# A hybrid attention and convolution block: later transposes of k and q tiles, and one filler part moved ahead of the attention

## The chip, the cores and the metric

One NeuronCore of a Trainium2 chip runs the whole program. The metric is device time in microseconds, the median of several executions of the same kernel. The engines are PE (matmuls and transposes; PEld loads its weights), DVE, ACT and POOL (vector work), and SP, whose queue issues all DMAs here.

## The reference, cut to what matters

One layer over 1024 tokens of width 1024. Everything is float32. The change lies in the first half, up to the output projection:

```python
h = rmsnorm(x, attn_norm)
q, k, v, conv_a, conv_g = split(h @ w_in)           # 512 columns each
q = rmsnorm(q.reshape(S, 4, 2, 64), q_norm)         # k likewise
o = diff_attention(q, k, v, lam)                    # 4 heads, two softmax maps each, ALiBi bias
attn_out = rmsnorm(o, head_norm) * (1 - lam_init)
conv_out = silu(layernorm(depthwise_conv31(conv_a * sigmoid(conv_g))))
x = x + concat([attn_out, conv_out]) @ w_out
# then a SwiGLU feed-forward part and a gated per-layer embedding, both added to x
```

## The kernel before, in words

Each float32 product is made of three matmuls on parts rounded to the PE's input format: high by high, low by high and high by low (`mm3`, lines 78 to 80). So every operand is split into a high and a low tile, the high one by ACT, the low one by DVE or POOL.

Tokens are worked on in 8 tiles of 128. The stages up to the attention are: a norm of x with transposes, v and a small projection of the per-layer embedding; the convolution channels (GLU, 31 taps, layer norm, swish), with the k projection beside their end; and the q projection, beside the layer norm of the convolution. `qk_proj` makes the k and the q tiles. For token tile t it does 24 matmuls into a PSUM tile `pk` or `pq`; ACT copies it to `nk` or `nq` and squares it; DVE sums the squares (`ssk`, `ssq`), POOL raises the sums to the power -1/2 (`rstd_of`, line 107), DVE multiplies; PE transposes the tile (`tk`, `tq`, line 376); ACT and DVE write the halves `qh` and `ql` (lines 379, 380); and two DMAs store them to DRAM, from where the attention loads them per head.

The attention has 16 parts: 4 heads by 2 halves of the queries by 2 pairs of query tiles. For a query tile, PE makes the scores of each of two maps (`s`, lines 562 to 565), DVE takes the negative maximum (`nm`), ACT the exponential (`e`, line 570), POOL combines the two maps (lines 578, 579), PE transposes the result in two halves (`wt`, line 584), ACT and DVE split it (`wth`, `wtl`), and PE multiplies it with v (`av`). Two PSUM tiles hold scores, two hold transposes. A head's result is normed by `head_norm` (transposes `hn` and `hb`), a head's half later.

The convolution's share of the output projection, `conv_out(i)`, fills PE between the attention's steps: 16 pieces `pc` of 12 matmuls each, for 2 column halves by 8 token tiles, each with a residual `pt` loaded from x, an addition and a store to `part_d`. Part i of the attention issues piece i, after its last scores. `conv_w` loads the weights (`wcr`) and splits them (`wch`, `wcl`). After the attention comes the projection of its own result, `po`, with the weights `wo`.

The order of instructions on each engine is fixed when the program is built, by a scheduler that goes by the order of the code, by priorities (`later`, `issue_after`) and by a modelled timeline; on the chip each engine takes its instructions in that order. `issue_after(x)` makes the instructions inside it eligible only once x has been issued.

Of the kernel before, what the change touches and what calls it, by code (L numbers as in the profile page):

```python
# [2 lines left out]

# [5 lines left out]
F32 = mybir.dt.float32  # L9
F32R = mybir.dt.float32r  # L10
BF16 = mybir.dt.bfloat16
AF = mybir.ActivationFunctionType
ALU = mybir.AluOpType
AX = mybir.AxisListType
# [3 lines left out]
P = 128  # L18
# [19 lines left out]
NVF = 4  # L38
ND = [23, 17, 17, 18]
OTB = 2  # L40
FSTART = 0
HNT = (0, 3)
NVL = 2
MV = (0, 0)
# [7 lines left out]
def hybrid_block(ctx: ExitStack, tc: tile.TileContext, I, out):  # L52
# [6 lines left out]
    def f32(ap):  # L59
        return ap.bitcast(F32)  # L60
# [15 lines left out]
    def mm3(ps, lh, ll, rh, rl, first, last, more=False):  # L76

        nc.tensor.matmul(ps, lh, rh, start=first, stop=False, skip_group_check=more)  # L78
        nc.tensor.matmul(ps, lh, rl, start=False, stop=False, skip_group_check=more)  # L79
        nc.tensor.matmul(ps, ll, rh, start=False, stop=last, skip_group_check=more)  # L80

    @contextmanager
    def later(n):
# [20 lines left out]
    def rstd_of(ms, n, pool, name):  # L104
        r = pool.tile([P, n], F32, name=name + "_r", tag="st_r", bufs=4)
        nc.vector.tensor_scalar_add(ms, ms, EPS)  # L106
        nc.gpsimd.tensor_tensor(r, ms, mhalf[:, 0:1].broadcast_to([P, n]), ALU.pow)  # L107
        return r
# [45 lines left out]
    def mm_tile(name):  # L154
        i = mmn[0] = (mmn[0] + 1) % mmn[1]
        if i < 2:
            return ps1.tile([P, 512], F32, name=name, tag=f"mm{i}", bufs=1)
        return psB.tile([P, 512], F32, name=name, tag=("av", "fl")[i - 2], bufs=1)
# [33 lines left out]
    def proj_tok(ps, t, ws):  # L192
        half, tt = t // 4, t % 4
        a = slice(tt * P, (tt + 1) * P)
        for k in range(KT):
            wh, wl = ws(k)
            mm3(ps, hT[half][k // 4][:, k % 4, a], lT[half][k // 4][:, k % 4, a], wh, wl, k == 0, k == KT - 1)

    wv_load, wv = w_set(rp1, [(wq[i], 2) for i in (0, 1, 2, 3)], w_in, 2 * CW, "wv", 3, nc.gpsimd)

# [121 lines left out]
    def conv_tile(j, ndve, delay):  # L322
# [19 lines left out]
        with later(delay):  # L342
# [13 lines left out]
                    nc.gpsimd.tensor_add(y2, y2, pr)  # L356
            nc.vector.tensor_add(y, acc, y2)

    def qk_proj(nm, c0, g, hd, ld, slots):
        load, ws = w_set(rp1, [(wq[i], 2) for i in slots], w_in, c0, "w" + nm, 3, nc.vector)  # L360
        for i in range(4):
            load(i)
        for t in range(NT):
            ps = mm_tile(f"p{nm}{t}")
            proj_tok(ps, t, ws)
            qn = p1m.tile([P, 8, HD], F32, name=f"n{nm}{t}", tag="sq", bufs=7)
            nc.scalar.copy(qn.rearrange("p a b -> p (a b)"), ps)
            sq = p1m.tile([P, 512], F32, name=f"sq{nm}{t}", tag="sq", bufs=7)
            nc.scalar.activation(sq, ps, AF.Square, scale=HD ** -0.5)
            ss = p1m.tile([P, 8], F32, name=f"ss{nm}{t}", tag="qss", bufs=4)  # L370
            nc.vector.tensor_reduce(ss, sq.rearrange("p (a b) -> p a b", b=HD), AX.X, ALU.add)
            r = rstd_of(ss, 8, p1m, f"r{nm}{t}")
            nc.vector.tensor_mul(qn, qn, r.unsqueeze(2).broadcast_to([P, 8, HD]))
            tp = tp_tile(f"t{nm}{t}")
            for h in range(NH):
                nc.tensor.transpose(tp[:, h, :], qn[:, 2 * h:2 * h + 2, :], ident)
            qh = nat.tile([P, NH, P], F32R, name=f"{nm}h{t}", tag="nat", bufs=6)
            ql = nat.tile([P, NH, P], F32R, name=f"{nm}l{t}", tag="nat", bufs=6)
            nc.scalar.activation(qh, tp, AF.Copy, scale=g)
            nc.vector.scalar_tensor_tensor(ql, tp, g, f32(qh), ALU.mult, ALU.subtract)  # L380
            for dst, src in ((hd, qh), (ld, ql)):
                c0 = t * P % dst[0].shape[1]
                dma(f32(dst[t // 4][:, c0:c0 + P]).rearrange("(h p) s -> p h s", p=P), f32(src))

    def conv_ln():

# [65 lines left out]
                split(wh[:, k, :], wl[:, k, :], raw, None, (nc.gpsimd, nc.vector)[ch == 0 and 2 * g + k in WV])  # L452
            woc.append((wh, wl))

    def conv_out(i):

        ch, t = i // NT, i % NT
        cs = slice(ch * 512, (ch + 1) * 512)
        if t == 0 and ch == 1:
            conv_w(1, otp, 2, "pt")  # L460
        pt = otp.tile([P, 512], F32, name=f"pt{ch}{t}", tag="pt", bufs=2)
        dma(pt, x[t * P:(t + 1) * P, cs])
        ps = psB.tile([P, 512], F32, name=f"pc{ch}{t}", tag="fl", bufs=1)
        a = slice(t % 4 * P, (t % 4 + 1) * P)
        for k in range(NCT):
            wh, wl = woc[k // 2]
            mm3(ps, mC[0][t // 4][:, k, a], mC[1][t // 4][:, k, a], wh[:, k % 2, :], wl[:, k % 2, :],
                k == 0, k == NCT - 1)
        nc.vector.tensor_add(pt, pt, ps)
        dma(part_d[t * P:(t + 1) * P, cs], pt)  # L470

    mmn[1] = QB
    qk_proj("q", 0, qg, qh_d, ql_d, (2, 3, 0, 1))
    conv_w(0, rp1, 3, "raw")
    es1.close()
    ps1.release()

# [44 lines left out]
    for h in range(NH):  # L522
# [11 lines left out]
        for c in range(2):  # L534
# [14 lines left out]
            for pr_ in range(2):  # L549
# [37 lines left out]
                    if pend and tt in HNT:  # L587
                        next(pend[0], None)
                fi = h * 4 + c * 2 + pr_ - FSTART
                if fi >= 0:  # L590
                    n = 16 - fi if h * 4 + c * 2 + pr_ == 15 else 1
                    with tc.issue_after(s_mm.ins), later(FDELAY):
                        for i in range(fi, fi + n):
                            conv_out(i)
# [495 lines left out]
```

## Time and profile before

| | us |
|---|---|
| median of 3 executions (lowest, highest) | 1291.48 (1289.46, 1292.21) |
| the profiled execution, its own time | 1289.18 |
| the span of its trace | 1287.4 |
| PE busy in the span | 1249.3 |
| DVE, ACT, POOL busy | 937.5, 583.0, 394.4 |

The span leaves out 1.8 us of the profiled execution. The times in the rows below count from the start of the span. Conv pieces run from 292.7 to 476 us, the k products from 170.4 to 221, the q products from 223.5 to 279.

### The profile page before, as it was taken

How to read it: one execution, taken by the hardware profiler on the slowest of the kernel's cores; microseconds unless marked ns; L12 is line 12 of the kernel's file. 1: busy time of each engine (PE TensorE's matmuls, PEld its weight loads, DVE VectorE, ACT ScalarE, POOL GpSimd, SP SyncE). 2: the span in 40 equal slices, each digit the busy share in tenths (PEclk: the TensorE clock that was granted, in tenths of full speed). 3: DMA queues.
4: the chain of work that ended last, by engine and by line, in shares of the span. 5: the costliest groups of instructions: out<-in, count | busy, mean ns of one | idle time of the engine just before them, and what ended most of it. 6: DMA issues, size and time to landing. Idle time of an engine off the chain costs nothing.

```text
span 1287.4 us, 16537 instructions
## 1 busy us (share of the span) xinstructions
PE 1249.3 (97%) x5945; PEld 1021.1 (79%) x5945; DVE 937.5 (73%) x1220; ACT 583.0 (45%) x862; POOL 394.4 (31%) x237
## 2 busy tenths in 40 slices
PE   8999998989999999987999999999999999999998
PEld 6788877867887888866888888888888788888886
DVE  7548999868887885877667676667665576567797
ACT  7445565445776673442223232223232444346552
POOL 2459998576667661660000000000000000000230
PEclk9999999989999999988999999999999999999999
DMA  9731232496655243445444445444454997665445
GB/s 356 240 88 50 66 107 74 127 225 176 154 126 149 76 134 121 172 131 180 146 165 147 156 164 172 147 161 147 152 171 166 385 349 234 191 196 176 135 147 164
DMA packets 165079, 213.12 MB, mean 166 GB/s; under 512 B 12088, under 2 KB 90182, under 8 KB 164997
## 3 DMA queue, kind: packets, MB, share of 16 engines
q1 hardware_dynamic: 164996, 212.06, 52.0%
q8 instruction: 47, 0.77, 0.3%
q14 instruction: 36, 0.29, 0.1%
HBM read 146.41 MB, written 65.60 MB: 165 GB/s over the span
## 4 chain that ended last, share of the span: by engine, by line
PE 81%; DVE 7%; DMA 6%; issue 2%; POOL 2%; ACT 1%; SPq 1%; DVEq 0%; POOLq 0%; ACTq 0%
PE Y L78 5%; PE Y L79 5%; PE Y L80 5%; PE Z L79 3%; PE Z L78 3%; PE Z L80 3%; PE X L80 3%; PE X L78 3%; PE X L79 3%; PE dY L78 2%; PE dY L79 2%; PE dY L80 2%; PE s L562 2%; DVE acc L351 2%; PE s L563 2%
## 5 line engine op out<-in xcount | busy, mean ns | idle before, releaser
L107 POOL TENSOR_TENSOR n_r<-n_ss,mhalf 128x1 f32<-128x1 f32 x24 | 14.7, 617 | 670.1 <-DVE n_ss L106 661.6
L74 DVE TENSOR_TENSOR dl<-dr,dh 128x1024 fp32r<-128x1024 f32 x77 | 93.7, 1224 | 62.6 <-ACT dh L71 62.4
L71 ACT CAST dh<-dr 128x1024 fp32r<-128x1024 f32 x77 | 80.5, 1049 | 105.9 <-PE dY L80 37.2
L356 POOL TENSOR_TENSOR z<-z,pr 128x1024 f32<-128x1024 f32 x45 | 115.8, 2575 | 3.2 <-ACT pr L355 0.8
L351 DVE SCALAR_TENSOR_TENSOR acc<-u,cw,acc 128x1024 f32<-128x1024 f32 x71 | 91.2, 1285 | 1.5
L570 ACT ACTIVATE e<-s,nm 128x1024 f32<-128x1024 f32 x64 | 71.6, 1119 | 35.9 <-DVE nm L567 29.6
L567 DVE TENSOR_REDUCE nm<-s 128x1 f32<-128x1024 f32 x64 | 77.3, 1219 | 9.1 <-PE s L565 4.5
L579 POOL TENSOR_TENSOR e<-e,e 128x1024 f32<-128x1024 f32 x32 | 77.8, 2431 | 2.4
L355 ACT ACTIVATE pr<-u,cw 128x1024 f32<-128x1024 f32 x45 | 51.1, 1150 | 36.0 <-POOL z L356 35.6
L562 PE MATMUL s<-ka,qa 128*128 128x512 f32 x128 | 57.3, 448 | 1.6 <-ACT e L570 1.5
L578 POOL TENSOR_SCALAR e<-e,cf 128x1024 f32<-128x1024 f32 x32 | 36.9, 1153 | 65.0 <-DVE cf L577 31.9
L79 PE MATMUL dY<-dl,dh 128*128 128x512 f32 x132 | 51.5, 390 | 0.0
L563 PE MATMUL s<-kb,qb 80*128 80x512 f32 x128 | 51.4, 402 | 0.0
L80 PE MATMUL dY<-dh,dl 128*128 128x512 f32 x132 | 51.4, 389 | 0.0
L78 PE MATMUL dY<-dh 128*128 128x512 f32 x132 | 50.3, 391 | 0.0
L74 DVE TENSOR_TENSOR wtl<-wt,wth 128x512 fp32r<-128x512 f32 x64 | 43.2, 683 | 8.9 <-ACT wth L71 8.6
L71 ACT CAST wth<-wt 128x512 fp32r<-128x512 f32 x64 | 36.8, 587 | 20.6 <-PE wt L584 20.5
L796 DVE TENSOR_TENSOR aa<-Z,aa 128x512 f32<-128x512 f32 x22 | 15.2, 690 | 38.5 <-PE Z L80 38.3
L80 PE MATMUL X<-B11h,a11l 128*128 128x512 f32 x88 | 33.5, 401 | 6.5 <-DVE a11l L74 6.5
L79 PE MATMUL av<-wtl,avh 128*128 128x256 f32 x128 | 38.4, 300 | 0.0
L584 PE MATMUL wt<-ident,e 128*128 128x128 f32 x256 | 37.5, 273 | 0.3 <-DVE wtl L74 0.2
L78 PE MATMUL av<-wth,avh 128*128 128x256 f32 x128 | 37.5, 293 | 0.2 <-ACT wth L71 0.2
(396 smaller groups left out, 3984.9 us busy)
## 6 DMA issues: line engine op xcount, KB each, us to landing
dr<-ga_d SPq DMA_DIRECT2D x77, 256.0 KB, 5.6
wr<-in_w_gate SPq DMA_DIRECT2D x44, 256.0 KB, 3.0
wr<-in_w_up SPq DMA_DIRECT2D x44, 256.0 KB, 3.5
wd<-in_w_down SPq DMA_DIRECT2D x22, 512.0 KB, 3.5
wb_d<-wd SPq DMA_DIRECT2D x44, 256.0 KB, 2.0
ga_d<-h SPq DMA_DIRECT2D x44, 256.0 KB, 3.6
dr<-wb_d SPq DMA_DIRECT2D x44, 256.0 KB, 3.4
dr<-in_w_down SPq DMA_DIRECT2D x33, 256.0 KB, 3.1
```

The costliest lines, as they stand in the source:

```text
L71: nc.scalar.copy(h, src)
L74: (eng_l or nc.vector).tensor_sub(l, src, f32(h))
L78: nc.tensor.matmul(ps, lh, rh, start=first, stop=False, skip_group_check=more)
L79: nc.tensor.matmul(ps, lh, rl, start=False, stop=False, skip_group_check=more)
L80: nc.tensor.matmul(ps, ll, rh, start=False, stop=last, skip_group_check=more)
L351: nc.vector.scalar_tensor_tensor(acc, u[:, k:k + S], cw[:, j, k:k + 1], acc, ALU.mult, ALU.add)
L356: nc.gpsimd.tensor_add(y2, y2, pr)
L562: nc.tensor.matmul(o, qa[:, m, ts_], ka[:, m, kc * 512:(kc + 1) * 512], start=True, stop=False)
L563: nc.tensor.matmul(o, qb[:, m, ts_], kb[:, m, kc * 512:(kc + 1) * 512], start=False, stop=not diag)
L567: nc.vector.tensor_reduce(nm, sp, AX.X, ALU.max, negate=True)
L570: nc.scalar.activation(e, sp, AF.Exp, bias=nm, accum_out=s)
L579: nc.gpsimd.tensor_add(es[0], es[0], es[1])
```

## The change

The transposes of a k or q tile, the two splits of them and the two stores become a function `turn`. It isn't called in the turn of its own tile: it is put on a list, and called inside `issue_after` behind the last matmul of a later tile, for k tiles behind two further tiles' products, for q tiles from the second on behind one. The last two k turns come with the first q tiles, and the last q turn comes behind `conv_out(0)`. Piece 0 of `conv_out` is issued before the attention, and its residual is loaded by a statement ahead of the q projection, into a tile of its own. Part i of the attention then issues piece i + 1, and the last part has none.

```diff
-FSTART = 0
+FSTART = -1
...
+    turns = []
+
     def qk_proj(nm, c0, g, hd, ld, slots):
...
-        for t in range(NT):
-            ps = mm_tile(f"p{nm}{t}")
-            proj_tok(ps, t, ws)
...
+        def turn(t, qn):
             tp = tp_tile(f"t{nm}{t}")
...
+        for t in range(NT):
+            ps = mm_tile(f"p{nm}{t}")
+            mm = proj_tok(ps, t, ws)
+            keep = 1 if nm == "k" or t == 0 else 0
+            with tc.issue_after(mm.ins):
+                while len(turns) > keep:
+                    turns.pop(0)()
...
+            turns.append(partial(turn, t, qn))
...
-    def conv_out(i):
+    def conv_out(i, pt=None):
...
-        pt = otp.tile([P, 512], F32, name=f"pt{ch}{t}", tag="pt", bufs=2)
-        dma(pt, x[t * P:(t + 1) * P, cs])
+        if pt is None:
+            pt = otp.tile([P, 512], F32, name=f"pt{ch}{t}", tag="pt", bufs=2)
+            dma(pt, x[t * P:(t + 1) * P, cs])
...
+    pt0 = p1m.tile([P, 512], F32, name="pt00", tag="pt0")
+    dma(pt0, x[0:P, 0:512])
     qk_proj("q", 0, qg, qh_d, ql_d, (2, 3, 0, 1))
     conv_w(0, rp1, 3, "raw")
+    mm = conv_out(0, pt0)
+    with tc.issue_after(mm.ins):
+        turns.pop(0)()
...
-                if fi >= 0:
+                if fi < 16:
```

What this does to the order on the engines is shown at two places. In the names, the digits behind `nq`, `tq`, `qh` are the token tile; those behind `s`, `nm`, `e` are head, query tile and map; those behind `pc` are column half and token tile; those behind `wt` are head, query tile and half; the number after the underscore is a buffer.

**End of the q projection.** PE before, from the transposes of q tile 5 on:

```order
L376 MATMUL tq5_2466<-ident_86,nq5_2456 128x128 x4
L80 MATMUL pq7_2523<-wq3_h_2197,lT11_142 128x512
L376 MATMUL tq6_2512<-ident_86,nq6_2502 128x128 x4
L562 MATMUL s000_2662<-ka0_2641,qa00_2650 128x512
...
L562 MATMUL s001_2673<-ka0_2641,qa00_2650 128x512
...
L376 MATMUL tq7_2558<-ident_86,nq7_2548 128x128 x4
L562 MATMUL s011_2716<-ka0_2641,qa00_2650 128x512
...
L78 MATMUL pc00_2750<-wch00_2569,mCh0_2157 128x512
```

PE in the changed kernel:

```order
L370 MATMUL tq5_2493<-ident_86,nq5_2458 128x128 x4
L80 MATMUL pq7_2514<-wq3_l_2178,hT11_138 128x512
L81 MATMUL pq7_2514<-wq3_h_2177,lT11_142 128x512
L79 MATMUL pc00_2580<-wch00_2560,mCh0_2135 128x512
...
L370 MATMUL tq6_2539<-ident_86,nq6_2504 128x128 x4
L581 MATMUL s000_2679<-ka0_2658,qa00_2667 128x512
...
L370 MATMUL tq7_2595<-ident_86,nq7_2550 128x128 x4
L581 MATMUL s010_2722<-ka0_2658,qa00_2667 128x512
...
L79 MATMUL pc01_2767<-wch00_2560,mCh0_2135 128x512
```

Piece `pc00` moved ahead of the transposes of q tile 6, the transposes of q tile 7 ahead of the third score tile `s010`, and `pc01` stands where `pc00` stood.

ACT before, from the squares of q tile 7 on:

```order
L369 ACTIVATE sqq7_2550<-pq7_2523 128x512
L379 ACTIVATE qh6_2517<-tq6_2512,qg_706 128x512
L570 ACT_TABLE_LOAD
L570 ACTIVATE e000_2670,sm000_2671<-s000_2662,nm000_2668 128x1024
L570 ACTIVATE e001_2681,sm001_2682<-s001_2673,nm001_2679 128x1024
L379 ACTIVATE qh7_2563<-tq7_2558,qg_706 128x512
L570 ACTIVATE e010_2713,sm010_2714<-s010_2705,nm010_2711 128x1024
```

ACT in the changed kernel:

```order
L390 ACTIVATE sqq7_2552<-pq7_2514 128x512
L373 ACTIVATE qh6_2544<-tq6_2539,qg_706 128x512
L373 ACTIVATE qh7_2600<-tq7_2595,qg_706 128x512
L589 ACT_TABLE_LOAD
L589 ACTIVATE e000_2687,sm000_2688<-s000_2679,nm000_2685 128x1024
L589 ACTIVATE e001_2698,sm001_2699<-s001_2690,nm001_2696 128x1024
L589 ACTIVATE e010_2730,sm010_2731<-s010_2722,nm010_2728 128x1024
```

`qh7` moved ahead of the table load and of the first two exponentials. DVE before, from the sum of squares of q tile 7 on:

```order
L371 TENSOR_REDUCE ssq7_2552<-sqq7_2550 128x8
L380 SCALAR_TENSOR_TENSOR ql6_2518<-tq6_2512,qg_706,qh6_2517 128x512
L106 TENSOR_SCALAR ssq7_2552<-ssq7_2552 128x8
L567 TENSOR_REDUCE nm000_2668<-s000_2662 128x1
L567 TENSOR_REDUCE nm001_2679<-s001_2673 128x1
L373 TENSOR_TENSOR nq7_2548<-nq7_2548,rq7_r_2554 128x512
```

DVE in the changed kernel:

```order
L392 TENSOR_REDUCE ssq7_2554<-sqq7_2552 128x8
L107 TENSOR_SCALAR ssq7_2554<-ssq7_2554 128x8
L482 TENSOR_TENSOR pt00_2155<-pt00_2155,pc00_2580 128x512
L374 SCALAR_TENSOR_TENSOR ql6_2545<-tq6_2539,qg_706,qh6_2544 128x512
L394 TENSOR_TENSOR nq7_2550<-nq7_2550,rq7_r_2556 128x512
L586 TENSOR_REDUCE nm000_2685<-s000_2679 128x1
L586 TENSOR_REDUCE nm001_2696<-s001_2690 128x1
L374 SCALAR_TENSOR_TENSOR ql7_2601<-tq7_2595,qg_706,qh7_2600 128x512
```

The scaling of q tile 7 moved ahead of the two maxima, and the addition of piece 0 came in between.

**Last part of the attention.** PE before, from the end of the last score tile `s371` on:

```order
L565 MATMUL s371_4985<-distb_732,identb_730 128x128
L78 MATMUL pc17_5026<-wch10_3959,mCh1_2159 128x512
...
L80 MATMUL pc17_5026<-wch11_3969,mCl1_2160 128x512
L501 MATMUL hn30_4823<-ident_86,ot30_4821 128x128 x4
L584 MATMUL wt350_4873<-ident_86,e350_4852 128x128 x4
L78 MATMUL po00_5306<-wo00_h_5272,mAh0_2637 128x512
...
L584 MATMUL wt351_4880<-ident_86,e350_4852 128x128 x4
...
L78 MATMUL av31_4904<-wth310_4776,avh3_4465 128x256
...
L584 MATMUL wt360_4960<-ident_86,e360_4939 128x128 x4
```

PE in the changed kernel:

```order
L584 MATMUL s371_5002<-distb_732,identb_730 128x128
L520 MATMUL hn30_4840<-ident_86,ot30_4838 128x128 x4
L603 MATMUL wt350_4890<-ident_86,e350_4869 128x128 x4
L603 MATMUL wt351_4897<-ident_86,e350_4869 128x128 x4
L79 MATMUL av31_4921<-wth310_4793,avh3_4482 128x256
L79 MATMUL po00_5306<-wo00_h_5272,mAh0_2654 128x512
...
L603 MATMUL wt360_4977<-ident_86,e360_4956 128x128 x4
```

`pc17` is gone from behind the scores, and the second half of the transposes, `wt351`, and the first `av31` moved ahead of the first matmuls of `po`. In the k stage, the rows of PE are the same in both kernels up to the first q products, so the transposes of k tiles 0 to 5 stand where they stood. On SP, the load of the residual `pt00` moved to the beginning of the program, behind the load of x tile 3.

## Rows read from the trace of the kernel before

**Rows 1.** Page: busy time of the matmul engine; GB/s moved in 40 slices.
```profile
PE 1249.3 (97%) x5945; PEld 1021.1 (79%) x5945; DVE 937.5 (73%) x1220; ACT 583.0 (45%) x862; POOL 394.4 (31%) x237
...
GB/s 356 240 88 50 66 107 74 127 225 176 154 126 149 76 134 121 172 131 180 146 165 147 156 164 172 147 161 147 152 171 166 385 349 234 191 196 176 135 147 164
```

**Rows 2.** Waits of PE, whole span: engine, line, releaser: us, times, longest.
```profile
PE tq L376 <- DVE nq L373: 5.0, 1, 5.0
...
PE tk L376 <- DVE nk L373: 3.8, 4, 1.4
...
PE s L562 <- ACT e L570: 1.5, 2, 0.9
...
PE pc L78 <- ACT wch L71: 1.2, 1, 1.2
...
PE hb L516 <- DVE wtl L74: 0.8, 2, 0.4
```

**Rows 3.** Three stretches: us, busy (x count) of PE, PEld, DVE, ACT, POOL; PEclk, DMA, GB/s.
```profile
279.00:284.00 5.00, 0.16 (x1) 0.00 (x0) 2.00 (x5) 2.78 (x6) 1.64 (x1) 0.77 1.05 235
...
552.00:556.00 4.00, 1.27 (x9) 0.83 (x8) 4.00 (x5) 3.81 (x8) 0.23 (x1) 0.84 0.00 0
...
556.00:560.00 4.00, 4.00 (x10) 2.88 (x11) 4.00 (x5) 2.53 (x3) 4.00 (x2) 0.50 0.63 215
```

**Rows 4.** Timeline, last q tiles: start us, us, engine, line, operation [idle before <-releaser].
```profile
278.62 0.62 ACT L71 CAST wch<-wcr 128x512 fp32r<-128x512 f32 x1 [6.00 <-DMA wcr<-in_w_out]
...
281.70 1.64 POOL L107 TENSOR_TENSOR rq_r<-ssq,mhalf 128x8 f32<-128x8 f32 x1 [4.49 <-DVE ssq L106]
...
283.37 0.69 DVE L373 TENSOR_TENSOR nq<-nq,rq_r 128x512 f32<-128x512 f32 x1 [1.75 <-POOL rq_r L107]
...
283.98 0.74 DVE L380 SCALAR_TENSOR_TENSOR ql<-tq,qg,qh 128x512 fp32r<-128x512 f32 x1
...
284.21 1.09 PE L376 MATMUL tq<-ident,nq 128*128 128x128 f32 x4 [5.05 <-DVE nq L373]
...
284.64 0.68 DVE L371 TENSOR_REDUCE ssq<-sqq 128x8 f32<-128x512 f32 x1
...
286.04 1.28 ACT L570 ACT_TABLE_LOAD   x1
...
288.55 1.11 ACT L570 ACTIVATE e<-s,nm 128x1024 f32<-128x1024 f32 x1 [1.22 <-DVE nm L567]
...
289.80 0.51 PE L562 MATMUL s<-ka,qa 128*128 128x512 f32 x1 [0.87 <-ACT e L570]
...
291.67 0.69 ACT L379 ACTIVATE qh<-tq,qg 128x512 fp32r<-128x512 f32 x1 [0.23 <-ACT e L570]
...
292.67 0.40 PE L78 MATMUL pc<-wch,mCh 128*128 128x512 f32 x1
```

**Rows 5.** Timeline, ACT alone, around its table load in the conv normalisation.
```profile
250.61 1.28 ACT L410 ACT_TABLE_LOAD   x1
251.91 1.45 ACT L410 ACTIVATE y<-ytb,cols 128x512 f32<-128x512 f32 x2
```

**Rows 6.** Timeline, last part of the attention.
```profile
473.25 0.47 PE L78 MATMUL pc<-wch,mCh 128*128 128x512 f32 x1
...
473.40 1.06 ACT L71 CAST wo_h<-wo_raw 128x1024 fp32r<-128x1024 f32 x1 [0.75 <-PE s L563]
...
473.54 0.68 DVE L74 TENSOR_TENSOR wtl<-wt,wth 128x512 fp32r<-128x512 f32 x1
...
474.37 1.11 ACT L570 ACTIVATE e<-s,nm 128x1024 f32<-128x1024 f32 x1
...
476.10 0.60 PE L501 MATMUL hn<-ident,ot 128*128 128x128 f32 x4
...
477.50 0.58 ACT L503 COPY on<-hn 128x512 f32<-128x512 f32 x1
...
478.91 0.60 ACT L71 CAST wth<-wt 128x512 fp32r<-128x512 f32 x1
```

More of the change, by code (lines that the diff above doesn't have):

```diff
@@ L1 @@
 import math
+from functools import partial
 from contextlib import ExitStack, contextmanager
@@ L79, in mm3 @@
         nc.tensor.matmul(ps, lh, rl, start=False, stop=False, skip_group_check=more)
-        nc.tensor.matmul(ps, ll, rh, start=False, stop=last, skip_group_check=more)
+        return nc.tensor.matmul(ps, ll, rh, start=False, stop=last, skip_group_check=more)
     @contextmanager
@@ L196, in proj_tok @@
             wh, wl = ws(k)
-            mm3(ps, hT[half][k // 4][:, k % 4, a], lT[half][k // 4][:, k % 4, a], wh, wl, k == 0, k == KT - 1)
+            mm = mm3(ps, hT[half][k // 4][:, k % 4, a], lT[half][k // 4][:, k % 4, a], wh, wl, k == 0, k == KT - 1)
+        return mm
     wv_load, wv = w_set(rp1, [(wq[i], 2) for i in (0, 1, 2, 3)], w_in, 2 * CW, "wv", 3, nc.gpsimd)
@@ L362, in qk_proj @@
             load(i)
-        for t in range(NT):
-            ps = mm_tile(f"p{nm}{t}")
-            proj_tok(ps, t, ws)
[L366 to L373, printed above, removed]
+        def turn(t, qn):
             tp = tp_tile(f"t{nm}{t}")
@@ L383, in qk_proj @@
                 dma(f32(dst[t // 4][:, c0:c0 + P]).rearrange("(h p) s -> p h s", p=P), f32(src))
+        for t in range(NT):
[5 more added lines that the diff above has]
+                    turns.pop(0)()
+            qn = p1m.tile([P, 8, HD], F32, name=f"n{nm}{t}", tag="sq", bufs=7)
+            nc.scalar.copy(qn.rearrange("p a b -> p (a b)"), ps)
+            sq = p1m.tile([P, 512], F32, name=f"sq{nm}{t}", tag="sq", bufs=7)
+            nc.scalar.activation(sq, ps, AF.Square, scale=HD ** -0.5)
+            ss = p1m.tile([P, 8], F32, name=f"ss{nm}{t}", tag="qss", bufs=4)
+            nc.vector.tensor_reduce(ss, sq.rearrange("p (a b) -> p a b", b=HD), AX.X, ALU.add)
+            r = rstd_of(ss, 8, p1m, f"r{nm}{t}")
+            nc.vector.tensor_mul(qn, qn, r.unsqueeze(2).broadcast_to([P, 8, HD]))
+            turns.append(partial(turn, t, qn))
     def conv_ln():
@@ L466, in conv_out @@
             wh, wl = woc[k // 2]
-            mm3(ps, mC[0][t // 4][:, k, a], mC[1][t // 4][:, k, a], wh[:, k % 2, :], wl[:, k % 2, :],
-                k == 0, k == NCT - 1)
+            mm = mm3(ps, mC[0][t // 4][:, k, a], mC[1][t // 4][:, k, a], wh[:, k % 2, :], wl[:, k % 2, :],
+                     k == 0, k == NCT - 1)
         nc.vector.tensor_add(pt, pt, ps)
         dma(part_d[t * P:(t + 1) * P, cs], pt)
+        return mm
     mmn[1] = QB
+    pt0 = p1m.tile([P, 512], F32, name="pt00", tag="pt0")
+    dma(pt0, x[0:P, 0:512])
     qk_proj("q", 0, qg, qh_d, ql_d, (2, 3, 0, 1))
     conv_w(0, rp1, 3, "raw")
+    mm = conv_out(0, pt0)
+    with tc.issue_after(mm.ins):
+        turns.pop(0)()
     es1.close()
```

## Prediction

> **What bounds the kernel now.** I read the page first, then the waits of PE, the timeline at the two places where the order changes, and three stretches with the granted clock. PE is busy for 1249.3 of 1287.4 us [rows 1], so it bounds the kernel, and a change can win only PE's idle time, or time at a low clock. Of PE's waits the ones within reach are these [rows 2]: 5.0 us before the transposes of a q tile, once; 3.8 us before those of k tiles, in four pieces; 1.5 us for exponentials; 1.2 us for the weights of a conv piece; 0.8 us before `hb`, in two.
>
> The 5.0 us stand at 279.2 to 284.2 and begin on another engine. ACT sits idle for 6.00 us until the last weight tile `wcr` has landed, and casts it at 278.62. Only behind that, in its queue, come the copy and the squares of q tile 6; POOL has the power at 281.70 to 283.34, DVE scales at 283.37, and PE gets its transposes at 284.21 [rows 4]. In this wait the granted clock fell: 0.77 over 279 to 284 us with PE busy for 0.16 us, which is a mix of the two levels [rows 3]. The low level (1.2 GHz) shows in 556 to 560: 10 matmuls in 4 us at 0.50, behind a stretch with PE busy for 1.27 of 4 us. At the high level (2.4 GHz) a piece `pc` of 12 takes 2.85 us, from 473.25 to the `hn` behind it at 476.10 [rows 6], 0.24 us each, so 4 us would hold 17. Four microseconds at the low level cost (17 - 10) x 0.24 = 1.7 us.
>
> **The later turns.** For k the scheduler had already moved the transposes behind later products: the rows of PE are the same in both kernels up to the first q products. So the 3.8 us stay. I take 0. For q the transposes were interleaved already too; tiles 0 to 5 move by a few matmuls while PE had other products, 0 again. What counts is tiles 6 and 7.
>
> **The piece ahead of the attention.** No work is added or removed; 12 matmuls move into the wait. PE is free at 284.21 - 5.05 = 279.16. The piece needs the last weight too, but as its last quarter only: high part at 279.24, low part some 0.7 us later. So it runs from 279.2 to 282.0 without a stop. The low part of that weight now stands ahead of the sum of squares of tile 6 on DVE instead of behind, so I put the transposes of tile 6 at 283.7, 0.5 earlier. 1.7 us of the wait remain.
>
> Now what is late next. In the new order ACT does `qh7` before the table load and the first exponential. `qh7` hangs on q tile 7: behind the scaling of tile 6, which ends at 283.5, DVE does a `ql` (0.74) and a sum of squares (0.68), POOL a power (1.64), DVE a scaling (0.69) [rows 4], together 3.75, and with an addition of a constant some 3.9: 287.4. The transposes (0.60, as `hn` in [rows 6]) bring 288.2, `qh7` (0.69) 288.9, the table load (1.28) 290.2. In the trace the load ran at 286.04, long before the first exponential at 288.55, which waited for its maximum. It loses its cover, and the exponential moves by 1.65 us. The third score tile needs the PSUM tile that this exponential reads: it started 1.25 us behind it, at 289.80, and will at 291.45. PE has nothing else in its order there, so it idles for 3.3 us from 288.1, where pieces were meant to help. Behind it the fourth score tile waits for the second exponential, 1.2 us after the first (1.11 and a read of the sum), and ends at 293.6, where before the piece came at 292.67. From there on PE is 0.95 us behind, with one piece more done, and since it hardly waits in the attention, the lag stays. Bounds: -1.0 (tile 6 earlier by more, as the landing of the weight has a spread I can't see) to +2.0.
>
> The Trainium skill has a rule on the load. Its page "ScalarE: Activation LUTs" ("What ACT_TABLE_LOAD costs") adds a drain of about 1.38 us to a load of about 1.28. The trace shows the load with 1.28 us and the next activation at 251.91, right at its end [rows 5], so the measurement differs from the page and my sum leaves the drain out; by the page the lag would be an estimated 2.3 instead of 0.95 us.
>
> **The clock at this place.** From 286.3, when the two score tiles end, to 291.45 PE has only the transposes of tile 7, so the clock will fall as it did at 279 to 284 and 552 to 556 [rows 3]. In the kernel before, the fall hit the first two score tiles. Here it is later, and it can reach the third and fourth score tile and `pc01`. Between 0 (over before 291.45) and 1.7 us; I take the middle, +0.85.
>
> **Pieces one part earlier.** Parts 0 to 14 do the next piece, 12 matmuls for 12 matmuls: 0. The first piece with the second half's weights comes one part earlier, cut up between other work; whether its wait of 1.2 us [rows 2] goes is open, since the weights are asked for earlier too. Between -1.2 and +1.2, taken at -0.6, as the cut leaves the weights more time.
>
> **The last part without a piece.** There 2.85 us of PE work go, and what was behind them? Before, PE had the piece at 473.25, `hn` at 476.10 and the projection `po` from 476.9. In the change `hn` comes at 473.25. The first half `wt350` needs a PSUM tile that DVE frees at 473.54 + 0.68: 474.25. The second half `wt351` now directly follows and needs the tile that `hn` fills, which ACT empties behind a cast of `wo` (473.40) and an exponential (474.37 + 1.2) by a copy of 0.58 [rows 6]: 476.1. The first `av` needs the cast of `wt350`, behind another cast of `wo` (1.06): 476.1 + 1.06 + 0.60 = 477.7. PE is in order, so `po`, which could run, waits: it begins at 477.8 instead of 476.9, with 0.56 us of the other work done (half a `wt` and an `av`). So +0.35 us: the piece's time isn't won, it turns into three waits of 0.5, 1.4 and 1.1 us. Against that, `po` now stands between the last transposes and `av`, and `hb`, where one of the two waits for `hb` was lost, 0.4 at most [rows 2]: -0.4. Together -0.05; bounds -2.85 (all of it won) to +0.35.
>
> **The clock there.** From 473.7 to 477.8 PE would be busy for about 1 of 4 us, as little as in 552 to 556, where the clock fell. Behind that PE runs without a gap, so a fall would cost in full: 0 to 1.7 us, taken at +0.85.
>
> **The early residual.** 256 KB more in the first 35 us, at the page's 356 GB/s of the first slice [rows 1] 0.74 us of transfer, in front of x tiles 4 to 7. PE is busy there with the embedding's projection; I take 0, and 0.74 as the upper end, -0.5 as the lower, since the order of transposes and products there is new too.
>
> **Sum.** 0.95 + 0.85 - 0.6 - 0.05 + 0.85 + 0 = +2.0 us. On the profiled execution's 1289.18 (its span of 1287.4 and 1.8 around it) that is 1291.2. The median of the runs lies 2.3 above that execution, so the forecast for the median is 1291.48 + 2.0 = 1293.5. About 0.2% (2.6 us) is what a measurement of this kernel can tell from no change, so it is no change, leaning slower.
>
> **Rivals.**
> 1. The wait is filled and nothing is late behind it: tile 7 is ready soon enough that the exponential starts where it did, and PE runs ahead with `po` at the end. Then the piece's 2.85 us are won, with 0.6 of the waits for exponentials and 1.2 for weights: 1291.48 - 4.6 = 1286.9. For it speaks that the wait of 5.0 us is real and longer than the piece; against it the rows of ACT, where `qh7` stands first, and those of PE at the end.
> 2. The clock falls at both new gaps and stays low over running work: slower. It decides once the two falls together outlast the gaps by the work of more than about 2 us. 0.95 + 1.7 + 1.7, with the early residual at 0.74, `wch` at 0 and the end at +0.35: +5.4, 1296.9. For it speaks that both gaps are as empty as the ones behind which it fell [rows 3]; against it that at the first place part of the low time passes while PE waits anyhow.
> 3. The change does nothing, because the scheduler had the same order: true for k, not for the two places.
>
> **How the numbers follow.** The forecast, within 0.2%, has 0.42. Slower by more has 0.35: rival 2, the cases where one clock term is full and the weights' wait grows, and 0.05 for a table load that holds ACT longer than its row. Faster by more has 0.23: rival 1 and the lower bounds of the first lag together with the end. The third rival is inside the forecast. The range reaches to both rivals: 1286.9 to 1296.6. The likeliest case's own range is 1290.7 to 1295.7.
>
> **What would show it.** Right: the first wait for `tq` at about 1.7 us; the first exponential behind `qh7` and the table load, some 1.6 us later; a wait of 3 us of `s` for that exponential; at the end three waits of PE before `wt`, `wt` and `av` of 3 us together; a granted clock of 0.5 behind one gap or both. Wrong: an exponential that starts before 289 us, `po` running within a microsecond after the last scores, or waits of PE in the first 60 us that grew by over 1 us.

## The result, and the profile after

The change makes the kernel slower. Median 1300.4 us (1296.59 to 1301.41, 5 runs) against 1291.48 us (1289.35 to 1292.21, 5 runs) of the kernel before: ratio 1.0076, 95% interval 1.0061 to 1.0090. The forecast was 1293.5 with a range of 1286.9 to 1296.6, so the time lies 3.8 us above the range. The profiled execution took 1300.4 us, with a span of 1298.6 against 1287.4, 11.2 us more; the medians are 8.9 apart, as the profiled execution of the kernel before (1289.18) lies 2.3 below its median.

The page has the same work on PE and the same bytes moved, so the loss is waiting and clock, not work; busy PE grows by 4.7 us against [rows 1], as matmuls at the low clock are busy for longer:

```profile
PE 1254.0 (97%) x5945; PEld 1024.0 (79%) x5945; DVE 938.9 (72%) x1220; ACT 582.6 (45%) x862; POOL 390.9 (30%) x237
```

The waits of PE, as in [rows 2] (engine, line, what it waits for: us in total, times, longest):

```profile
PE X L81 <- DVE a11l L75: 9.1, 1, 9.1
PE s L581 <- ACT e L589: 6.3, 3, 3.3
...
PE tk L370 <- DVE nk L394: 3.8, 4, 1.3
PE pc L79 <- DVE pt L482: 1.9, 1, 1.9
PE tq L370 <- DVE nq L394: 1.7, 1, 1.7
...
PE wt L603 <- ACT on L522: 1.1, 1, 1.1
...
PE av L79 <- ACT wth L72: 0.8, 1, 0.8
...
PE wt L603 <- DVE wtl L75: 0.5, 1, 0.5
```

The kernel before had this in place of the first row:

```profile
PE X L80 <- DVE a11l L74: 6.5, 1, 6.5
```

`X` and `Y` are products of the feed-forward part, behind the attention. The wait there is 2.6 us longer, but that is not 2.6 us of loss: just ahead of it (573 to 583 us) PE is only 7.5 us later than before, and behind it 10.0, against 9.7 at the first `Y`.

The wait ahead of the q transposes fell from 5.0 to 1.7, as forecast; that of the k transposes is 3.8 as before. Waits for exponentials grew from 1.5 to 6.3 in all, and a wait of 1.9 is new: a piece `pc` that waits for DVE's addition `pt` of the piece ahead of it.

At which point of the attention the time is lost shows when the same matmul is compared in both timelines. Taken is the start of the last matmul of a score tile (64 of them, numbered from 0, 4 to each part), and elsewhere the start of the named matmuls:

| place | before, us | after, us | later by |
|---|---|---|---|
| transposes of k tile 5 (`tk`) | 222.85 | 222.60 | -0.25 |
| score tile 4 (part 1) | 296.27 | 300.38 | 4.1 |
| score tile 30 (part 7) | 373.34 | 377.62 | 4.3 |
| score tile 31 (part 7) | 374.42 | 381.83 | 7.4 |
| score tile 63 (part 15) | 473.21 | 481.14 | 7.9 |
| last `hn` transposes | 497.59 | 506.16 | 8.6 |
| first `Y` of the products behind | 555.74 | 565.44 | 9.7 |
| end of the span | 1287.4 | 1298.6 | 11.2 |

Three jumps stand in the attention: 4.3 at its start, 3.1 at one tile of part 7, 0.6 at its end. Behind it, 1.1 us come before `Y`, where the low clock lies otherwise over the same waits, and 1.35 in the first down products (`dX`), with waits for `dh` casts; both are in one execution, and no run here takes them apart.

**The start.** The timeline that answers to [rows 4] (start us, us, engine, line, operation [idle before <-releaser]):

```profile
278.23 0.62 ACT L72 CAST wch<-wcr 128x512 fp32r<-128x512 f32 x1 [5.90 <-DMA wcr<-in_w_out]
...
280.83 1.63 POOL L108 TENSOR_TENSOR rq_r<-ssq,mhalf 128x8 f32<-128x8 f32 x1 [3.91 <-DVE ssq L107]
...
283.34 0.63 PE L370 MATMUL tq<-ident,nq 128*128 128x128 f32 x4 [1.73 <-DVE nq L394]
...
288.24 0.69 ACT L373 ACTIVATE qh<-tq,qg 128x512 fp32r<-128x512 f32 x1 [3.55 <-DVE nm L586]
288.94 1.28 ACT L589 ACT_TABLE_LOAD   x1
290.24 1.11 ACT L589 ACTIVATE e<-s,nm 128x1024 f32<-128x1024 f32 x1
...
291.50 0.79 PE L581 MATMUL s<-ka,qa 128*128 128x512 f32 x1 [3.29 <-ACT e L589]
```

The forecast's late links are there: `qh7` ahead of the table load, the first exponential at 290.24 (forecast 290.2), the third score tile at 291.50 (forecast 291.45), behind a wait of 3.29 us (forecast 3.3). The early links came out by luck: the transposes of tile 6 start 0.36 us before the forecast's 283.7 and the scaling of tile 7 ends 0.3 before its 287.4, but the transposes of tile 7 then take 0.97 us at the low clock instead of 0.60. The exponential follows the load at once: 288.94 + 1.28 = 290.22, and it starts at 290.24. The Trainium skill ("ScalarE: Activation LUTs", "What ACT_TABLE_LOAD costs") adds a drain of about 1.38 us to each switch; the load stands on the critical chain here, and no such time is there.

Five stretches with the granted clock, as in [rows 3] (window, us, busy us (x count) of PE, PEld, DVE, ACT, POOL; PEclk, DMA share, GB/s):

```profile
279.00:284.00 5.00, 3.27 (x17) 2.52 (x16) 2.98 (x6) 2.38 (x5) 1.63 (x1) 1.00 1.02 220
284.00:291.00 7.00, 4.20 (x14) 2.29 (x12) 5.48 (x8) 3.42 (x4) 1.63 (x1) 0.76 1.10 233
291.00:298.00 7.00, 6.50 (x16) 4.59 (x17) 3.12 (x6) 3.69 (x7) 3.48 (x2) 0.53 0.96 297
380.00:384.00 4.00, 3.99 (x11) 2.90 (x12) 3.92 (x7) 2.63 (x5) 3.28 (x2) 0.57 0.21 51
486.00:490.00 4.00, 4.00 (x12) 3.10 (x11) 3.42 (x7) 4.00 (x11) 2.55 (x2) 0.58 0.71 247
```

The kernel before, in two of the same stretches:

```profile
291.00:298.00 7.00, 7.00 (x36) 5.20 (x35) 5.63 (x11) 3.57 (x8) 4.64 (x3) 1.00 0.95 300
380.00:384.00 4.00, 4.00 (x30) 3.46 (x30) 3.78 (x7) 3.97 (x10) 3.35 (x2) 1.00 1.01 223
```

While the piece fills 279 to 284 the clock stays high. It falls twice behind it: in 284 to 291, where a wait follows anyhow, and, after full clock from 288 to 291 with PE waiting, again in nearly all of 291 to 298, where PE has work without a gap: 0.53 of full speed, mostly the level of 1.2 GHz, and 6.50 us busy, by estimate worth 6.50 x 0.47 = 3.1 us. So the 4.1 us at the start are the forecast's lag of 0.95 and a fall of about 3.1, not of 0.85. It isn't one odd execution: w2_behind_e and resid_first below, with the same orders at this place, show waits of 3.30 and 3.29 us for the exponential and a granted clock of 0.57 and 0.53 over 291 to 298. It falls again behind the new waits at 380 and at 486. The Trainium skill ("TensorE: Matmul & The Clock Gate", "Terms") prices time under the throttle with that time x (1 - granted share), an estimate of 3.3 for these 7 us; the table agrees, with 4.1 - 0.95 = 3.15.

**Part 7.** The rows of ACT, PE, SP and DVE there:

```profile
375.79 0.62 ACT L72 CAST wch<-wcr 128x512 fp32r<-128x512 f32 x1 [1.79 <-DMA wcr<-in_w_out]
377.75 0.62 ACT L72 CAST wch<-wcr 128x512 fp32r<-128x512 f32 x1 [1.34 <-DMA wcr<-in_w_out]
...
380.01 0.74 PE L581 MATMUL s<-ka,qa 128*128 128x512 f32 x1 [2.17 <-ACT e L589]
...
381.63 0.58 SPq L559 DMA_DIRECT2D qa<-qh_d  x1
...
387.80 0.83 SPq L475 DMA_DIRECT2D pt<-in_x  x2
...
396.65 0.69 DVE L482 TENSOR_TENSOR pt<-pt,pc 128x512 f32<-128x512 f32 x1 [2.51 <-issue]
...
397.39 0.50 PE L79 MATMUL pc<-wch,mCh 128*128 128x512 f32 x1 [1.90 <-DVE pt L482]
```

Two casts of the second half's weights wait on ACT for their DMA, and the exponential that score tile 31 needs stands behind them; that is the jump of 3.1, of which 2.17 is the wait and the rest low clock. Then the residuals of pieces 8 and 9 are asked for only at 387.80, behind the next head's queries and keys on SP. The queries themselves were issued only at 381.63, with the last matmuls of score tile 31 (381.40 and 381.83): SP had waited 4.0 us for PE's scores, so what holds up that tile holds up the residuals too. DVE adds piece 8 at 396.65 (the profile names no releaser there), and piece 9, which needs its PSUM tile, waits until 397.39. These rows look like two causes; the experiments ask which of them counts.

**The end**, answering to [rows 6]:

```profile
481.21 0.61 PE L520 MATMUL hn<-ident,ot 128*128 128x128 f32 x4
482.30 0.63 PE L603 MATMUL wt<-ident,e 128*128 128x128 f32 x4 [0.49 <-DVE wtl L75]
484.01 0.66 PE L603 MATMUL wt<-ident,e 128*128 128x128 f32 x4 [1.08 <-ACT on L522]
485.44 0.39 PE L79 MATMUL av<-wth,avh 128*128 128x256 f32 x1 [0.78 <-ACT wth L72]
485.67 0.41 PE L79 MATMUL po<-wo_h,mAh 128*128 128x512 f32 x1
```

The three forecast waits are there, with 0.49, 1.08 and 0.78 us (forecast 0.5, 1.4, 1.1), and eat nearly all of the 2.85 us of the piece that is missing here.

### The profile page after: what moved, and what is told of

Read it like the earlier page. It is cut to its first block, busy times and chain, and to the rows that moved or that the text cites. A ratio compares the mean times of both kernels' runs of the same rounds, so it can differ in the third digit from the quotient of the medians.

```text
span 1298.6 us, 16539 instructions
## 1 busy us (share of the span) xinstructions
PE 1254.0 (97%) x5945; PEld 1024.0 (79%) x5945; DVE 938.9 (72%) x1220; ACT 582.6 (45%) x862; POOL 390.9 (30%) x237
## 4 chain that ended last, share of the span: by engine, by line
PE 78%; DVE 10%; DMA 5%; issue 3%; POOL 2%; ACT 1%; SPq 1%; DVEq 0%; POOLq 0%; ACTq 0%
PE Y L79 4%; PE Y L80 4%; PE Y L81 4%; PE Z L80 3%; PE Z L79 3%; PE Z L81 3%; PE X L81 3%; PE X L79 3%; PE X L80 3%; PE dY L81 2%; PE dY L80 2%; PE dY L79 2%; PE s L581 2%; DVE acc L353 2%; PE s L582 2%
```

## The experiments

Ten kernels were run, each beside the kernel before on the same chip. The median of the kernel before moved by up to a microsecond from one set of runs to the next, so kernels of different sets are compared by their ratios (0.001 is 1.3 us). A difference of two ratios is uncertain by some 0.002, about 2.4 us (an estimate from their intervals). The first theory, A, was read off the rows above: `qh7` at the start, the casts in part 7, the end. Its rivals and successors are named in the expectations.

| kernel | median, us | before, us | ratio, 95% interval |
|---|---|---|---|
| the change | 1300.4 | 1291.48 | 1.0076 (1.0061 to 1.0090) |
| turns_only | 1289.15 | 1291.91 | 0.9979 (0.9965 to 0.9992) |
| filler_only | 1294.39 | 1291.91 | 1.0027 (1.0012 to 1.0042) |
| turn7_late | 1296.69 | 1291.91 | 1.0042 (1.0026 to 1.0058) |
| w2_behind_e | 1300.28 | 1291.91 | 1.0062 (1.0044 to 1.0079) |
| t7_resid_first | 1290.74 | 1290.86 | 1.0001 (0.9989 to 1.0014) |
| t7_skip7 | 1290.07 | 1290.86 | 0.9987 (0.9974 to 1.0000) |
| resid_first | 1292.64 | 1290.76 | 1.0015 (1.0003 to 1.0027) |
| turns_cast_late | 1286.52 | 1290.86 | 0.9969 (0.9955 to 0.9982) |
| turns_cast_late_w2_first | 1294.73 | 1290.86 | 1.0032 (1.0021 to 1.0044) |
| turns_cast_late_pt_first | 1285.73 | 1290.76 | 0.9960 (0.9947 to 0.9973) |

**turns_only**: one half of the change.

```diff
-FSTART = -1
+FSTART = 0
...
-    pt0 = p1m.tile([P, 512], F32, name="pt00", tag="pt0")
-    dma(pt0, x[0:P, 0:512])
...
-    mm = conv_out(0, pt0)
-    with tc.issue_after(mm.ins):
-        turns.pop(0)()
+    turns.pop(0)()
```

> The change with its queue of transposes alone: no piece ahead of the attention, none moved, no early residual. Theory A (the loss is not in the transposes but in three places that the moved piece makes: the first exponential behind qh7 and the table load, +4.6 us; the casts of the second half's weights ahead of an exponential in part 7, +3.1; the end, +0.6): ACT has qh7 behind two exponentials and the casts where they stood before, so all three are gone: 1291.5, within 1.5, and a wait for the tq transposes of about 5 us. Rival B (the queued transposes delay the q tiles, and all behind them): at least 3 us above 1291.5, with the first score later than the 285.0 us of before.

Faster than before by 0.21%, where theory A had no gain and B a loss. The queued transposes cost nothing; they help. Theory B falls. Rows of ACT and PE:

```profile
277.54 0.62 ACT L72 CAST wch<-wcr 128x512 fp32r<-128x512 f32 x1 [5.18 <-DMA wcr<-in_w_out]
...
282.65 0.94 PE L370 MATMUL tq<-ident,nq 128*128 128x128 f32 x4 [3.74 <-DVE nq L394]
```

The wait is 3.74 and not 5.05 us. On DVE the low part of that weight stands ahead of the sum of squares of tile 6 here, not between it and the constant that is added to it (0.6 us in the chain before), and the weight landed 1.1 us earlier; the granted clock is 0.50 from 283 to 286 us, and 0.50 from 282 to 288 in the kernel before. That these rows make the whole gain was not tried apart.

**filler_only**: the other half, on the kernel before.

```diff
-FSTART = 0
+FSTART = -1
...
     mmn[1] = QB
+    pt0 = p1m.tile([P, 512], F32, name="pt00", tag="pt0")
+    dma(pt0, x[0:P, 0:512])
...
     conv_w(0, rp1, 3, "raw")
+    conv_out(0, pt0)
```

> The kernel before with the piece ahead of the attention, the early residual and each piece one part earlier, but with the transposes where they were traced before. On ACT qh7 stands here behind the table load and the first exponential, ahead of the second. Theory A: the table load is hidden again, the second exponential alone is late (about +1.5 of the 4.6 us remain), the casts in part 7 (+3.1) and the end (+0.6) stay: 1296.7, with a wait of about 2 us for an exponential near 380 us. Rival B: without the queued transposes the piece fills the wait of 5 us and is won: 1288.6 or less.

Slower by 0.27%: between the theories in size, on the side of A in sign. The start is mild here, as expected (score tile 12 is 2.45 us later than before, with 2.85 us more work done). The loss is elsewhere than A had it: the wait for an exponential near 376 us is 0.58 us, and this stands instead:

```profile
284.27 0.63 PE L376 MATMUL tq<-ident,nq 128*128 128x128 f32 x4 [1.88 <-DVE nq L373]
...
394.39 0.79 PE L78 MATMUL pc<-wch,mCh 128*128 128x512 f32 x1 [3.93 <-DVE pt L470]
```

That points away from the casts on ACT and to the residual of piece 8. Theory A's wait of 2 us near 380 isn't there.

**turn7_late**: the change, with `qh7` behind two exponentials again.

```diff
-    with tc.issue_after(mm.ins):
-        turns.pop(0)()
+    turns.pop(0)()
...
+                        if h == 0 and 2 * t + m == T7AT:
+                            tc.add_manual_dep(last_t[1].ins, s_mm.ins.name, mybir.DependencyInfo(
+                                mybir.DependencyClass.NoSync, mybir.DependencyReason.DATA), reason="turn7")
```

`T7AT` is 2, the third score tile; the dependency sets an order and no wait.

> The change with one order altered: the transposes of q tile 7 stand on PE behind the first five matmuls of the third score tile, as before the change; ACT then does table load, two exponentials, qh7. Theory A: the wait of 3.3 us for the exponential at 288 to 291.5 falls to under 1 us, and with it most of the low clock behind it: -3.5 us, 1296.9; the wait of 2.2 us near 380 stays. Rival C (the low clock at this place comes from the gap ahead of the q transposes, whatever the order behind it): the wait goes, but the clock falls again and half or more of the gain is lost: 1299 or more.

1296.69, the time of theory A to 0.2 us (3.7 below the change by the medians, 4.4 by the ratios). The last matmul of score tile 4 is 1.7 us later than before instead of 4.1. But the wait did not fall to under 1 us: it is 1.88. The exponential starts at 288.98 instead of 290.24, 1.3 us earlier, and no sooner, as its maximum stands on DVE behind the scaling of q tile 7:

```profile
288.98 1.11 ACT L595 ACTIVATE e<-s,nm 128x1024 f32<-128x1024 f32 x1 [2.27 <-DVE nm L592]
...
290.24 0.50 PE L584 MATMUL s<-ka,qa 128*128 128x512 f32 x1 [1.88 <-ACT e L595]
...
383.80 0.83 SPq L479 DMA_DIRECT2D pt<-in_x  x2
...
393.95 0.80 PE L80 MATMUL pc<-wch,mCh 128*128 128x512 f32 x1 [3.45 <-DVE pt L486]
```

In t7_resid_first and t7_skip7 below, with the same order here, PE comes to the same wait earlier and stands 3.43 us. So the gap has two makers, ACT's order and DVE's, and only the first was changed. The scheduler also reordered some later work of the attention, so 4.4 us is the price of the edit and not of the one order alone.

What remains is in part 8. The residuals are asked for 4.0 us earlier than in the change, and piece 9 starts 3.4 us earlier; PE comes there earlier still, and waits longer.

**w2_behind_e**: the change, with the casts of the second half's weights behind the last exponential of part 7.

```diff
-            conv_w(1, otp, 2, "pt")
+            with tc.issue_after(last_e[0].ins):
+                conv_w(1, otp, 2, "pt")
```

> The change with one order altered: the four casts of the second half's weights are queued on ACT behind the last exponential of part 7, where the change has two of them, which wait 1.79 and 1.34 us for their DMA, ahead of an exponential that the next score tile needs. Theory A: the wait of 2.2 us at 380 and the low clock behind it go: -3.1 us, 1297.3, and the weights' lateness is taken up by other work, as piece 8 is cut up more. Rival D (the weights are late whoever waits; PE then stands before piece 8 instead): a wait of pc for wch of 2 us or more, 1300 within 1.

No gain: 1300.28. The wait for the exponential went, and a longer one of the piece came:

```profile
395.99 0.80 PE L79 MATMUL pc<-wch,mCh 128*128 128x512 f32 x1 [4.72 <-ACT wch L72]
```

D's forecast holds, and A's 1297.3 did not come. That the casts cost something in the change is not refuted by it, though: with the casts later, the two buffers come free later, and SP asks for the last two weights only at 385.66 and 387.76, behind the next head's loads (in the change at 375.20 and 377.80, ahead of them). The edit made a lateness of its own. It led to the next theory: the residuals of pieces 8 and 9 (here the weights too) come late because 2.3 MB for the next head (queries `qa` twice and `qb`, 256 KB each, keys `ka` twice and `kb`, 512 KB each), wanted a part or more later, stand ahead of them on SP.

**t7_resid_first**, on turn7_late, and **resid_first**, on the change: the same edit. `last_pt` is the load of the residual of piece 9.

```diff
-        dma(f32(ka[0:HD]), khs)
+        with behind(h == 3):
+            dma(f32(ka[0:HD]), khs)
...
-            dma(f32(qa[0:HD]), qhs)
+            with behind(h == 2 and c == 1):
+                dma(f32(qa[0:HD]), qhs)
...
+    def behind(on):
+        return tc.issue_after(last_pt[0].ins) if on else nullcontext()
```

> turn7_late (1296.7) with one order on SP altered: the loads of the residuals of pieces 8 and 9 stand ahead of the loads of the next head's keys and queries (qa of head 2, ka and kb of head 3), which are wanted only a part or more later. Theory E (piece 9 waits 3.45 us for the PSUM tile of piece 8, which DVE can't empty before the residual of piece 8 has landed; it stands behind some 2 MB of keys and queries on the queue, and one part earlier than before this falls on PE): the wait goes, and the low clock of 3.4 us behind it: -3.5 to -5, 1292.5. Rival F (the second half's weights themselves are late, as their raw tiles share two buffers with the residuals): the wait moves to wch or stays above 2 us: 1295 or more. The wait for an exponential at 376 us (1.56) is touched by neither.

1290.74: theory E, with 5.3 us below turn7_late by the ratios. The two traces show where: score tile 31 is equally late in both (3.2 and 3.3 us), score tile 63 is 6.0 us later than before in turn7_late and 0.9 here. No piece waits any more; the wait for an exponential at 376 us is still there with 1.70 us, and costs little.

> The change itself (1300.4) with the SP order of t7_resid_first alone: the residuals of pieces 8 and 9 are asked for ahead of the next head's keys and queries; qh7 stays ahead of the first exponential. With turn7_late (-3.6) and t7_resid_first (-9.7 both) it completes a square. Theory J (two independent losses): -6, 1294.5. Rival K (the loads cost only what their wait shows in the change, 1.90 us, since PE comes there later by the first loss; the rest of the 6 us was the low clock): 1298.

1292.64, 7.9 us below the change by the ratios. J's 6 lies within the uncertainty, and K falls. Rows of SP and DVE in resid_first:

```profile
378.48 5.96 SPq L479 DMA_DIRECT2D pt<-in_x  x2
...
387.64 0.68 DVE L488 TENSOR_TENSOR pt<-pt,pc 128x512 f32<-128x512 f32 x1
```

The residual of piece 8 is asked for 9.3 us earlier than in the change, and piece 8 is added 9.0 us earlier. Not all of the 7.9 us is traced to that. Between the two traces 2.2 us lie at score tile 31, where ACT's two casts wait 0.55 and 0.70 us in place of 1.79 and 1.34, though ACT and SP have the same order up to there: this seems to belong to the execution and not to the edit. 2.8 us follow up to tile 63, where the wait of 1.90 is gone, and 3.7 behind the attention, which no run takes apart. With turn7_late the four kernels make a square, by the ratios: the loads alone give back 7.9 us, `qh7` alone 4.4, both 9.7. Whether the two overlap by 2.6 or not at all the intervals leave open.

**t7_skip7**: turn7_late with no piece in part 7.

```diff
-                fi = h * 4 + c * 2 + pr_ - FSTART
-                if fi < 16:
-                    n = 16 - fi if h * 4 + c * 2 + pr_ == 15 else 1
+                part = h * 4 + c * 2 + pr_
+                fi = part + 1 if part < 7 else part
+                if part != 7:
...
+                        conv_out(fi)
```

> turn7_late (1296.7) with no piece in part 7: pieces 1 to 7 in parts 0 to 6, pieces 8 to 15 in parts 8 to 15, so the last part has a piece again and the second half's weights have the time that they had before. Theory E and F alike: the waits of pc near 394 go (-4), and those of wt, wt and av at 480 to 484 (2.4 us, with nothing gained, as the piece's 2.85 us of work return there): 1292, with at most a little more waiting in part 7, which has no piece. Rival G (the loss is spread, it comes from the piece ahead of the attention by itself): 1295 or more.

1290.07, as E and F had it; G falls. With the second half's pieces at their old places nothing is left of the loss, while the piece ahead of the attention is still there. So, with `qh7` behind two exponentials, that piece does no harm by itself, only by what follows one part early. It wins nothing either: turns_only, which has no piece there, is at 0.9979.

**turns_cast_late**: no piece at all in the wait; what made it is moved.

```diff
-                split(wh[:, k, :], wl[:, k, :], raw, None, (nc.gpsimd, nc.vector)[ch == 0 and 2 * g + k in WV])
+                with tc.issue_after(last_sq[0].ins) if ch == 0 and 2 * g + k == 3 else nullcontext():
+                    split(wh[:, k, :], wl[:, k, :], raw, None, (nc.gpsimd, nc.vector)[ch == 0 and 2 * g + k in WV])
```

> turns_only (1289.2) with one order altered: the cast of the last weight tile of the first half, for whose DMA ACT stands idle 5.2 us ahead of the copies and squares of q tiles 6 and 7, is queued behind the squares of tile 7. Theory H (the wait of 3.7 us for the q transposes is this cast; no piece is needed to fill it): the transposes of tile 6 start within 1 us of the last product, the score tiles some 3 us earlier, the clock does not fall there: -3 to -4.5, 1285.5. Rival I (the chain copy, squares, power, scaling is as long as the wait, or the first exponential becomes the next limit): less than 1.5 us gained, 1288.

1286.52, 0.31% below the kernel before; below turns_only by 1.3 us by the ratios and 2.6 by the medians, so the time does not choose between H and I. The wait went, as H had it; a new one of 2.03 us for the first exponential stands behind, as I had it, and the clock falls there all the same (0.52 over 286 to 289 us), which H had excluded. Its profiled execution took 1290.3, at the upper end of its runs, and shows where a part was lost again:

```profile
280.65 0.63 PE L371 MATMUL tq<-ident,nq 128*128 128x128 f32 x4 [0.64 <-DVE nq L395]
...
285.73 0.50 PE L579 MATMUL s<-ka,qa 128*128 128x512 f32 x1 [2.03 <-ACT e L587]
...
295.86 0.69 DVE L484 TENSOR_TENSOR pt<-pt,pc 128x512 f32<-128x512 f32 x1 [2.37 <-DMA pt<-in_x]
...
298.43 0.83 PE L601 MATMUL wt<-ident,e 128*128 128x128 f32 x5 [2.52 <-DVE wtl L75]
```

A residual behind loads that aren't urgent, once more: this time that of piece 0 behind the keys and values of head 1.

**turns_cast_late_w2_first**: the loads of `qa` and of `ka`, `kb` (head 3) behind those of the second half's weights, with `behind` as above.

> turns_cast_late with one more order altered, on SP: the loads of qa of head 2's second half and of ka and kb of head 3 stand behind the four loads of the second half's weights in place of ahead of three of them. Theory E: the wait of pc for wch (1.0 us at 389) and of hb behind it (0.4) go: 1.4 us below turns_cast_late. Rival F: the weights still wait for their two buffers; no more than 0.5 us, either way.

8.2 us above turns_cast_late: neither theory. The weights' loads came earlier, and the scheduler then put their casts, and the addition of piece 8, earlier in their queues too. The residuals of pieces 8 and 9 are asked for at 392.57, behind the next head's queries and keys, and DVE stands idle ahead of the addition with a maximum queued behind it, for which an exponential and then a score tile wait:

```profile
392.57 1.13 SPq L481 DMA_DIRECT2D pt<-in_x  x2
...
401.15 0.69 DVE L488 TENSOR_TENSOR pt<-pt,pc 128x512 f32<-128x512 f32 x1 [5.32 <-issue]
...
404.33 0.80 PE L585 MATMUL s<-ka,qa 128*128 128x512 f32 x1 [5.39 <-ACT e L593]
```

The profile names no releaser of the addition; as the last matmul of piece 8 started at 394.13, the residual is what was missing. It is the change's own fault again, made by another edit: an order on one queue is not an edit of one queue here.

**turns_cast_late_pt_first**: the keys and values of head 1 behind the residual of piece 0; on the other engines every instruction stands where it stood.

```diff
+        with behind(h == 1):
...
+                with behind(h == 1):
```

> turns_cast_late (1286.5) with one order altered, on SP: the keys and values of head 1, wanted at about 327 us, are asked for behind the residual of piece 0. In turns_cast_late DVE stood idle for 2.4 us before that residual landed at 295.9, with a maximum and two subtractions queued behind it, and PE waited 2.5 us for them at 298.4. Theory L (these loads fill the DMA engines ahead of the residual): the wait goes, with the low clock behind it: -2 to -4, 1283.5. Rival M (DMA is the limit from 276 to 297 us whatever the order; another load is late in its place): between -0.5 and +2, with a new wait of PE for queries, keys or values before 330 us.

1285.73: the best of all, 0.40% below the kernel before, but not told apart from turns_cast_late, so L's 2 to 4 us did not come. DVE waits no longer for the residual. In the profiled execution (1290.7, again at the upper end) the queries of the part behind are late, as M had it:

```profile
305.61 0.47 PE L587 MATMUL s<-ka,qa 128*128 128x512 f32 x1 [1.21 <-DMA qa<-qh_d]
```

## Why the prediction was wrong

The mechanism at the start was right, and its price was not. From `qh7` to the third score tile the times hold within 0.1 us, in part by luck, as said above. The step that failed is the term for **the clock at this place**: 0.85, with 1.7 as its upper end, taken from one fall of 4 us in which PE was assumed to wait for a part. The clock was low for nearly 7 us of running work, about 3.1 us. The upper end, 1.7, was worked out for the 4 us of a stretch of [rows 3], not for as long as the low level lasted.

**Pieces one part earlier**, -0.6 with bounds of 1.2, is the step that failed in kind. It asked whether PE would still wait 1.2 us for the weights. It did not follow what each piece needs besides: its residual, its weights' raw tiles that share two buffers with the residuals, and what stands ahead of both on SP. One part earlier these loads meet those of the next head. Measured are 4.3 to 7.9 us between tiles 30 and 63, so +3.6 in this trace, and two causes share it. The residuals behind the next head's loads are shown by experiment: resid_first gains 7.9 us on the change and t7_resid_first 5.3 on turn7_late, and t7_skip7 loses nothing with the pieces back in place. The jump of 3.1 at tile 31 is ACT's casts waiting for the weights; no run takes it away by itself, and it is 0.5 in resid_first and 1.8 in turn7_late with the same loads up to there, so the size of 3.1 is that of one execution.

**The later turns** were put at 0. By turns_only they gain 0.21% (0.08 to 0.35), 2.7 us. The order of DVE at tiles 6 and 7 had been noted, but only for the piece's sake.

**The last part without a piece** and **the clock there** were right in their sum, +0.80 forecast and +0.64 in the table, with waits of 2.35 us in place of 3.0. That is luck in part: the granted clock of 0.58 over 486 to 490 us is worth some 1.7 us (4.00 x 0.42, an estimate), twice its term, so the rest gained about 1 where -0.05 was forecast. **The early residual** was right: nothing is later by the transposes of k tile 5.

**The rivals and the range.** Rival 2 had the right mechanism at both gaps, and there is a third gap in part 7; its 1296.9 was too low as its clock terms were, and as it put the pieces one part earlier at 0. The range ended at 1296.6, below that rival; the upper bounds of all terms together come to +7.7, 1299.2, still under the measured 1300.4. Rival 1 fell: the wait was filled, and nothing was won, as the first exponential became the limit. All the signs named for "right" came, the last three waits somewhat shorter; none of them looked at part 7.

By terms, in the profiled execution: 0.95 lag and 3.1 clock at the start (forecast 1.8), 3.6 (forecast -0.6), 0.6 (forecast 0.8), and 2.6 behind the attention, which nothing in the forecast had and which stay open. The medians hold 2.3 us less than this sum.

## What to carry to other kernels

Work that is moved earlier takes its loads with it: before pricing it, follow each of its inputs along the issuing queue and its buffers, and look at what is asked for ahead of it, above all at the border of two stages. A gap is best taken away at what makes it: here one cast that waited for its DMA in front of ready work on ACT; with it moved, and the transposes queued, the kernel is 0.31% faster, where filling the gap won nothing. (0.21% comes from the queued transposes; the cast's own share is not told apart from none by the times.) A new gap can cost twice, when the clock that falls there stays low over the work behind it.

## What the runs showed of the hardware that was not expected

A load of 256 KB issued behind 2.3 MB on the same queue was used 8.9 us after its issue (387.80 to 396.65, in the change), with DMA at 219 GB/s in that stretch; asked for ahead of them, in resid_first, the residual of piece 9 landed 2.7 us after its issue. Behind 288.2 to 291.5 us, in which PE did nothing, the clock was low for nearly 7 us of unbroken work: 16 matmuls in 291 to 298, where the kernel before did 36. Not every gap does that: in turns_cast_late_pt_first PE waited 2.20 us up to 295.53, and the granted clock stayed at 1.00 from 293 to 302 us.
